# LN1's first two features of the second half in a fixed VectorE order, and FFN2's last input difference behind LN2's last split

## The chip, the core and the metric

The kernel runs on one core of a Trainium2 chip. The core has a matrix engine (TensorE, PE in the profile; its weight loads are listed as PEld), a vector engine (VectorE, DVE), an activation engine (ScalarE, ACT), GpSimd (POOL), and a queue that issues transfers (SyncE, SP). Each engine works through its own list of instructions in order, and waits on semaphores for the others. The metric is the device time of one execution in microseconds (us); of several executions the median is taken.

## What is computed

One layer of a hybrid decoder trunk on 544 tokens: 512 of one prompt (the first 256 tokens are called the first half here, the other 256 with 32 sample tokens the second half, 288 columns) with a model width of 1024. All tokens share the weights.

```python
x = layer_norm(ALPHA * x + 0.5 * swiglu(x, p["ffn1_wg"], p["ffn1_wu"], p["ffn1_wd"]), p["ln1_g"], p["ln1_b"])
proj = x @ p["w_in"]
...
mix = jnp.concatenate([y_rwkv, y_conv], axis=-1) @ p["w_out"]
x = layer_norm(ALPHA * x + mix, p["ln2_g"], p["ln2_b"])
x = layer_norm(ALPHA * x + 0.5 * swiglu(x, p["ffn2_wg"], p["ffn2_wu"], p["ffn2_wd"]), p["ln3_g"], p["ln3_b"])
```

Between `proj` and `mix` stand a per-token recurrence over a matrix state in eight heads (RWKV-7), and a short gated convolution. `layer_norm` subtracts the mean over the width, divides by the standard deviation, multiplies by g and adds b.

## The kernel before

Activations lie with the width on the 128 partitions: eight tiles of 128 features, called features 0 to 7 here, each with 544 token columns. `z` is the residual in f32. Every f32 product is made of three passes on PE: an operand is split into a high part (`hi`, a copy that ACT rounds) and a low part (`lo`, the difference, on DVE), and PE multiplies weight-high by high, weight-high by low and weight-low by high. `split` (L139 to L141) makes both parts of an activation; `wsplit` (L134 to L137) does it for a weight. `xhl` holds both parts of the input of the next matrix product. `mm3` (L148 to L156) is the inner loop of such a product: for each feature k three matmuls (L152, L153, L154), 256 columns wide in the first half and 288 in the second.

The work around LN1: FFN1 ends, LN1 of the first half runs while PE is busy with FFN1, and LN1 of the second half runs while PE makes the first half of five projections. PE then goes on with the second half of the projections 0, 1, 2 and so on, which need `xhl` of the second half. In the compiled order PE interleaves the first three of them (three accumulators, `mm`), taking for each feature the three passes of each projection.

`layer_norm` (L215) works on one half. Its last part, for the second half of LN1 (`fine` and `both` are set), treats features 0 and 1 singly: a multiplication by the reciprocal deviation (L269), scale and shift on DVE (L270), then the `sink`, which splits the feature into `xhl` and writes z to DRAM (`to_x`, L302). Features 2 to 7 go in pairs: one multiplication for the pair (L275), scale and shift of the odd feature on DVE (L279) and of the even one on ACT (L281), then the sink.

LN2 of the second half has no single features. It runs while PE makes FFN2's first products, and FFN2's input differences (`Ffn.inputs`, L454) follow it on DVE: FFN2 uses a scheme of fewer block products, for which differences of blocks of `z` are formed (`nt1`, L463; `ta`, L464, L466 and L469) and split into `tv`. `nt1` for features 0 and 1 and for features 2 and 3 stand in `cpb`; both are split into `xhl` at the end.

After the projections the first head pair is prepared: `project` mixes each projection with that of the token before (L914, L918), `gates`, `square`, `norms` (L996 clamps the key norms `kq`), `decays` and `prep` follow, and `scores` multiplies the score products by masks (L1060).

What sets the order: the kernel is written as generators that yield what they cost; `weave` runs one of them and fills in pieces of others by factors in the table `FILL`. A scheduler then lays out each engine's list from the recorded instructions by their dependencies and costs. `after(a, b)` adds a dependency without a semaphore: a stands behind b in the order; `tc.issue_after` does the same for all that is recorded in its block.

## Time and profile before

| | |
|---|---|
| median of 3 runs | 1072.5 us (1072.36 to 1072.72) |
| profiled execution, whole | 1072.43 us |
| profiled execution, span from first to last instruction | 1070.7 us |
| mean granted TensorE clock | 0.998 |
| instructions | 22612 |
| LN1 of the second half, last part | about 387 to 395 us |
| first pair's preparation | about 405 to 431 us |
| LN2 of the second half and FFN2's inputs | about 712 to 745 us |

The profile is of one execution. A row of the timeline gives the start in us from the span's start, the duration in us, engine, line, operation, output and inputs by the program's names, the shape and how many such instructions; where an engine stood idle ahead of it, the brackets give for how long and which instruction on which engine ended it. Instructions that follow each other on an engine can overlap by a few hundredths. The ends of matmuls are modelled.

### The profile page before, as it was taken

The numbers are of one execution on the slowest core, as the hardware profiler recorded it, in microseconds if no ns is written. First come the engines' busy times: TensorE is split into PE (matmuls) and PEld (weight loads), VectorE is DVE, ScalarE is ACT, GpSimd is POOL, SyncE is SP. The second block draws the span as 40 slices with busy tenths as digits, with TensorE's granted clock in tenths as the row PEclk, the third lists the DMA queues.
The fourth block names the chain that finished last, engine by engine and source line by source line (L and its number), as shares of the span: only waits on it lengthen the run. The fifth ranks groups of instructions, "written<-read, shape, count | busy, mean of one in ns | idle before, by whom it ended". The sixth has DMA issues, their size and how long they took to land.

```text
span 1070.7 us, 22612 instructions
## 1 busy us (share of the span) xinstructions
PE 1050.7 (98%) x9178; PEld 1010.5 (94%) x9178; DVE 844.7 (79%) x1557; ACT 583.2 (54%) x1070; POOL 154.9 (14%) x273
## 2 busy tenths in 40 slices
PE   9999999999999999999999999999999999999997
PEld 8999999999999999899889988999999999999996
DVE  6797888979875777793578657988979888797757
ACT  5746555555553668654444435767555555555524
POOL 0111121211200022133101200001211212121000
PEclk9999999999999999999999999999999999999999
DMA  8558585676854233324145724434766848668512
GB/s 292 132 112 186 120 199 135 145 172 132 186 118 158 79 88 109 85 82 99 41 143 161 173 81 139 141 119 79 152 165 137 200 101 194 143 137 189 147 43 84
DMA packets 91528, 144.48 MB, mean 135 GB/s; under 512 B 34848, under 2 KB 52384, under 8 KB 91296
## 3 DMA queue, kind: packets, MB, share of 16 engines
q1 hardware_dynamic: 68144, 110.76, 34.2%
q0 software_dynamic: 22848, 31.72, 19.2%
q8 instruction: 72, 1.18, 0.4%
q10 hardware_dynamic: 432, 0.56, 0.2%
q14 instruction: 32, 0.26, 0.1%
HBM read 128.81 MB, written 9.75 MB: 129 GB/s over the span
## 4 chain that ended last, share of the span: by engine, by line
PE 76%; DVE 13%; ACT 7%; issue 2%; DMA 2%; POOL 0%; ACTq 0%; DVEq 0%; SPq 0%
PE mm L553 9%; PE mm L554 9%; PE mm L555 9%; PE sm L553 6%; PE sm L554 6%; PE sm L555 6%; PE mm L152 6%; PE mm L153 5%; PE mm L154 5%; DVE hhl L141 2%; ACT hl L135 2%; DVE hl L136 2%; PE sm L441 1%; PE sm L1166 1%; PE mm L784 1%
## 5 line engine op out<-in xcount | busy, mean ns | idle before, releaser
L136 DVE TENSOR_TENSOR hl<-raw,hl 128x1024 fp32r<-128x1024 f32 (+3 forms) x230 | 270.2, 1179 | 63.7 <-ACT hl L135 62.6
L135 ACT ACTIVATE hl<-raw 128x1024 fp32r<-128x1024 f32 (+3 forms) x230 | 232.9, 1020 | 69.7 <-DVE raw L519 43.5
L152 PE MATMUL mm<-xhl,hl 128*128 128x256 f32 (+1 forms) x704 | 209.2, 299 | 0.5 <-ACT xhl L140 0.5
L153 PE MATMUL mm<-xhl,hl 128*128 128x256 f32 (+1 forms) x704 | 203.0, 289 | 0.4 <-DVE xhl L141 0.4
L154 PE MATMUL mm<-xhl,hl 128*128 128x256 f32 (+1 forms) x704 | 202.0, 287 | 0.0
L152 PEld LDWEIGHTS mm<-xhl,hl 128*128 128x128 f32 x704 | 132.0, 188 | 6.9 <-issue 2.0
L153 PEld LDWEIGHTS mm<-xhl,hl 128*128 128x128 f32 x704 | 132.3, 188 | 2.7 <-issue 1.0
L154 PEld LDWEIGHTS mm<-xhl,hl 128*128 128x128 f32 x704 | 132.3, 188 | 0.3 <-issue 0.2
L555 PE MATMUL sm<-xhl,hl 128*128 128x272 f32 x432 | 125.2, 290 | 0.0
L554 PE MATMUL sm<-xhl,hl 128*128 128x272 f32 x432 | 124.4, 288 | 0.0
L553 PE MATMUL sm<-xhl,hl 128*128 128x272 f32 x432 | 124.1, 287 | 0.0
L553 PE MATMUL mm<-tv,hl 128*128 128x272 f32 x288 | 83.3, 289 | 0.3
L555 PE MATMUL mm<-tv,hl 128*128 128x272 f32 x288 | 83.4, 290 | 0.0
L554 PE MATMUL mm<-tv,hl 128*128 128x272 f32 x288 | 83.1, 288 | 0.0
L553 PEld LDWEIGHTS sm<-xhl,hl 128*128 128x128 f32 x432 | 81.4, 188 | 0.0
L554 PEld LDWEIGHTS sm<-xhl,hl 128*128 128x128 f32 x432 | 81.3, 188 | 0.0
L555 PEld LDWEIGHTS sm<-xhl,hl 128*128 128x128 f32 x432 | 81.2, 188 | 0.0
L532 POOL DMA_DIRECT2D raw<-in_wd x32 | 39.2, 1462 | 288.0 <-DVE hlb L141 225.2
L526 POOL DMA_DIRECT2D raw<-in_gu x36 | 43.3, 1203 | 203.5 <-DVE hlb L141 143.8
L553 PE MATMUL mm<-hhl,hl 128*128 128x272 f32 x192 | 56.4, 300 | 0.3
L554 PE MATMUL mm<-hhl,hl 128*128 128x272 f32 x192 | 55.9, 291 | 0.8 <-DVE hhl L141 0.2
L553 PEld LDWEIGHTS mm<-tv,hl 128*128 128x128 f32 x288 | 54.2, 188 | 1.9 <-ACT cpb L620 1.9
(416 smaller groups left out, 2716.0 us busy)
## 6 DMA issues: line engine op xcount, KB each, us to landing
raw<-in_gu SPq DMA_DIRECT2D x84, 512.0 KB, 4.5
raw<-in_gu POOLq DMA_DIRECT2D x36, 512.0 KB, 6.6
raw<-in_wd SPq DMA_DIRECT2D x32, 512.0 KB, 4.5
raw<-in_win SPq DMA_DIRECT2D x26, 512.0 KB, 3.6
raw<-in_wd POOLq DMA_DIRECT2D x32, 256.0 KB, 6.0
z<-sv POOLq DMA_DIRECT2D x16, 272.0 KB, 8.4
raw<-in_wo_c SPq DMA_DIRECT2D x8, 512.0 KB, 3.6
raw<-in_wd SPq DMA_DIRECT2D x8, 384.0 KB, 3.2
```

Source lines behind the costliest of these rows:

```text
L135: seen["hi"] = ACT.activation(hl[:, 0, a:b], raw[:, a:b], AF.Copy)
L136: seen["lo"] = DVE.tensor_tensor(hl[:, 1, a:b], raw[:, a:b], hl[:, 0, a:b].bitcast(F32), op=OP.subtract)
L141: return DVE.tensor_tensor(lo, x, hi.bitcast(F32), op=OP.subtract)
L152: PE.matmul(out, wh, src[:, 0, k, c0:c1], start=(start and i == 0), stop=False)
L153: PE.matmul(out, wh, src[:, 1, k, c0:c1], start=False, stop=False)
L154: seen["fill"] = PE.matmul(out, wl, src[:, 0, k, c0:c1], start=False, stop=(stop and i == n - 1))
L441: PE.matmul(o[i][h][:, :c1 - c0], block(hl, v, k), xhl[:, y, k, c0:c1], start=(k == 0 and j == 0), stop=(k == KD - 1 and j == 2), skip_gro ...
L526: POOL.dma_start(x.rearrange("p (s c) -> p s c", s=2), bass.AP(tensor=a11.tensor, offset=a11.offset, ap=[[2 * D, P], [P * 2 * D, 2], [1, 5 ...
L532: POOL.dma_start(four(x)[:, i], bass.AP(tensor=a11.tensor, offset=a11.offset, ap=[[DFF, P], [P * DFF, 2], [1, 256]]), accum_op=OP.add)
L553: PE.matmul(out, wh, src(0, i), start=(first and i == 0), stop=False, skip_group_check=True)
L554: PE.matmul(out, wh, src(1, i), start=False, stop=False, skip_group_check=True)
L555: PE.matmul(out, wl, src(0, i), start=False, stop=(i == n - 1), skip_group_check=True)
```

## The change

In the last part of `layer_norm`, features 0 and 1 are put into a fixed order on DVE: feature 1's multiplication behind feature 0's scale and shift, feature 0's low part behind feature 1's multiplication, and feature 1's scale and shift behind feature 0's low part. The multiplication of a pair (in LN1's second half, all three pairs) stands behind feature 1's low part. `split` in `to_x` now leaves its last low part in `seen["xlo"]`. In `Ffn.inputs` the difference of features 2 and 3 stands behind that low part; FFN1's inputs run before any is set, so only FFN2's are touched. No instruction is added or removed.

```diff
-    seen = dict(rs=None, hhl=None, pe=None, fill=None, uv=None, new=[], old=[])
+    seen = dict(xlo=None, rs=None, hhl=None, pe=None, fill=None, uv=None, new=[], old=[])
...
         yield 1200 if pair else 600
+        los = []
         for d in range(2 if fine else 0):
             x = z[:, d, c0:c1]
-            DVE.tensor_tensor(x, x, rs[:, :n], op=OP.mult)
-            DVE.tensor_scalar(x, x, col(gcol, d), col(bcol, d), op0=OP.mult, op1=OP.add)
+            m = DVE.tensor_tensor(x, x, rs[:, :n], op=OP.mult)
+            if d:
+                after(m, ts)
+                after(los[0], m)
+            ts = DVE.tensor_scalar(x, x, col(gcol, d), col(bcol, d), op0=OP.mult, op1=OP.add)
+            if d:
+                after(ts, los[0])
             sink(d, z[:, d:d + 1, c0:c1], c0, c1)
+            los.append(seen["xlo"])
             yield 850
         for d in range(2 if fine else 0, KD, 2):
             zz = z[:, d:d + 2, c0:c1]
-            DVE.tensor_tensor(zz, zz, rs[:, None, :n].to_broadcast([P, 2, n]), op=OP.mult)
+            m = DVE.tensor_tensor(zz, zz, rs[:, None, :n].to_broadcast([P, 2, n]), op=OP.mult)
+            if los:
+                after(m, los[1])
...
-            split(xhl[:, 0, d:d + w, c0:c1], xhl[:, 1, d:d + w, c0:c1], x)
+            seen["xlo"] = split(xhl[:, 0, d:d + w, c0:c1], xhl[:, 1, d:d + w, c0:c1], x)
...
-                DVE.tensor_tensor(n1, z11[:, ks], z12[:, ks], op=OP.subtract)
+                e = DVE.tensor_tensor(n1, z11[:, ks], z12[:, ks], op=OP.subtract)
+                if k and seen["xlo"] is not None:
+                    after(e, seen["xlo"])
```

The change adds lines, so a line behind L266 stands up to 11 lines later in the changed kernel (L269 and L270 become L270 and L274, L275 becomes L282, L279 becomes L288, L463 becomes L472, L914 becomes L925).

DVE's list in the last part of LN1's second half, from feature 0's multiplication on (`z<-z,cpb` a multiplication, `z<-z,vc` scale and shift, `xhl<-z,xhl` a low part; 288 is one feature, 2x288 a pair). Before:

```order
L269 TENSOR_TENSOR z<-z,cpb 128x288 x2
L270 TENSOR_SCALAR z<-z,vc 128x288 x2
L275 TENSOR_TENSOR z<-z,cpb 128x2x288
L141 TENSOR_TENSOR xhl<-z,xhl 128x288 x2
L279 TENSOR_SCALAR z<-z,vc 128x288
L914 SCALAR_TENSOR_TENSOR v<-pb,vc,dt 128x256
L275 TENSOR_TENSOR z<-z,cpb 128x2x288
L141 TENSOR_TENSOR xhl<-z,xhl 128x2x288
L279 TENSOR_SCALAR z<-z,vc 128x288
L275 TENSOR_TENSOR z<-z,cpb 128x2x288
L279 TENSOR_SCALAR z<-z,vc 128x288
L141 TENSOR_TENSOR xhl<-z,xhl 128x2x288 x2
```

And now:

```order
L270 TENSOR_TENSOR z<-z,cpb 128x288
L274 TENSOR_SCALAR z<-z,vc 128x288
L270 TENSOR_TENSOR z<-z,cpb 128x288
L141 TENSOR_TENSOR xhl<-z,xhl 128x288
L274 TENSOR_SCALAR z<-z,vc 128x288
L925 SCALAR_TENSOR_TENSOR v<-pb,vc,dt 128x256
L141 TENSOR_TENSOR xhl<-z,xhl 128x288
L282 TENSOR_TENSOR z<-z,cpb 128x2x288 x2
L288 TENSOR_SCALAR z<-z,vc 128x288 x2
L282 TENSOR_TENSOR z<-z,cpb 128x2x288
L141 TENSOR_TENSOR xhl<-z,xhl 128x2x288 x2
L288 TENSOR_SCALAR z<-z,vc 128x288
```

Feature 0's low part moves ahead of the first pair's multiplication, feature 1's scale and shift behind it, and all three pairs' multiplications behind feature 1's low part; two of them now follow each other, ahead of the first pair's scale and shift. On PE, in the three interleaved projections (`mm_4547`, `mm_4554`, `mm_4619`), the matmuls that stand ahead of the first one on features 2 and 3 before (the second row that waits for ACT; the row that waits for DVE is the first on feature 2's low part):

```order
L153 MATMUL mm_4554<-xhl_68,hl_4354 128x288
L154 MATMUL mm_4554<-xhl_68,hl_4354 128x288
L152 MATMUL mm_4619<-xhl_68,hl_4397 128x288 [waits Activation_49]
L152 MATMUL mm_4547<-xhl_68,hl_4313 128x288 [waits Activation_49]
L152 MATMUL mm_4554<-xhl_68,hl_4354 128x288
L153 MATMUL mm_4619<-xhl_68,hl_4397 128x288
L154 MATMUL mm_4619<-xhl_68,hl_4397 128x288
L152 MATMUL mm_4619<-xhl_68,hl_4397 128x288
L153 MATMUL mm_4619<-xhl_68,hl_4397 128x288
L154 MATMUL mm_4619<-xhl_68,hl_4397 128x288
L152 MATMUL mm_4619<-xhl_68,hl_4397 128x288
L153 MATMUL mm_4547<-xhl_68,hl_4313 128x288 [waits DVE_49]
```

And now (the first row waits for feature 1's high part, the last but one for that of features 2 and 3):

```order
L152 MATMUL mm_4547<-xhl_68,hl_4313 128x288 [waits Activation_49]
L152 MATMUL mm_4554<-xhl_68,hl_4354 128x288
L154 MATMUL mm_4619<-xhl_68,hl_4397 128x288
L152 MATMUL mm_4619<-xhl_68,hl_4397 128x288
L153 MATMUL mm_4547<-xhl_68,hl_4313 128x288 [waits DVE_49]
L154 MATMUL mm_4547<-xhl_68,hl_4313 128x288
L153 MATMUL mm_4554<-xhl_68,hl_4354 128x288
L154 MATMUL mm_4554<-xhl_68,hl_4354 128x288
L153 MATMUL mm_4619<-xhl_68,hl_4397 128x288
L154 MATMUL mm_4619<-xhl_68,hl_4397 128x288
L152 MATMUL mm_4547<-xhl_68,hl_4313 128x288 [waits Activation_49]
L152 MATMUL mm_4554<-xhl_68,hl_4354 128x288
```

Now all 18 matmuls on features 0 and 1 stand ahead of the first on feature 2; before, the third projection's were taken partly behind it.

DVE's list in the preparation of the first head pair, before:

```order
L1005 SCALAR_TENSOR_TENSOR Pn<-keepm,sw 128x576
L996 TENSOR_SCALAR kq<-sm 128x256
L996 TENSOR_SCALAR kq<-sm 128x320
L914 SCALAR_TENSOR_TENSOR v<-pb,vc,dt 128x256
L918 SCALAR_TENSOR_TENSOR v<-pb,vc,dt 128x32
L1033 TENSOR_TENSOR AR_4714<-r,Pi 128x8x64
L1034 TENSOR_TENSOR AR_4714<-r,Pi 128x64
```

And now:

```order
L1016 SCALAR_TENSOR_TENSOR Pn<-keepm,sw 128x576
L1007 TENSOR_SCALAR kq<-sm 128x256
L925 SCALAR_TENSOR_TENSOR v<-pb,vc,dt 128x256
L929 SCALAR_TENSOR_TENSOR v<-pb,vc,dt 128x32
L1007 TENSOR_SCALAR kq<-sm 128x320
L1044 TENSOR_TENSOR AR_4714<-r,Pi 128x8x64
L1045 TENSOR_TENSOR AR_4714<-r,Pi 128x64
```

The second clamp of `kq` moves from ahead of the mixing of `v` to behind it, next to `AR`. The square of the keys that feeds these norms also moves ahead by a few instructions on ACT.

DVE's list at the end of LN2's second half (`cpb<-z` is the difference `nt1`; before, the first of the two is that of features 2 and 3). Before:

```order
L141 TENSOR_TENSOR xhl<-z,xhl 128x2x288
L279 TENSOR_SCALAR z<-z,vc 128x288 x2
L275 TENSOR_TENSOR z<-z,cpb 128x2x288
L463 TENSOR_TENSOR cpb<-z 128x544
L279 TENSOR_SCALAR z<-z,vc 128x288
L463 TENSOR_TENSOR cpb<-z 128x544
L141 TENSOR_TENSOR xhl<-z,xhl 128x2x288 x2
L405 TENSOR_TENSOR sv<-sv,mm 128x256
L141 TENSOR_TENSOR xhl<-z,xhl 128x2x288
L464 SCALAR_TENSOR_TENSOR cpb<-cpb,z 128x544
L141 TENSOR_TENSOR hlb<-raw,hlb 128x512
L141 TENSOR_TENSOR tv<-cpb,tv 128x544
```

And now:

```order
L141 TENSOR_TENSOR xhl<-z,xhl 128x2x288
L288 TENSOR_SCALAR z<-z,vc 128x288 x2
L282 TENSOR_TENSOR z<-z,cpb 128x2x288
L288 TENSOR_SCALAR z<-z,vc 128x288
L472 TENSOR_TENSOR cpb<-z 128x544
L141 TENSOR_TENSOR xhl<-z,xhl 128x2x288 x2
L414 TENSOR_TENSOR sv<-sv,mm 128x256
L141 TENSOR_TENSOR xhl<-z,xhl 128x2x288
L475 SCALAR_TENSOR_TENSOR cpb<-cpb,z 128x544
L141 TENSOR_TENSOR hlb<-raw,hlb 128x512
L472 TENSOR_TENSOR cpb<-z 128x544
L141 TENSOR_TENSOR tv<-cpb,tv 128x544
```

The difference of features 2 and 3 moves from ahead of three low parts and a scale and shift to behind the last low part and two more instructions, next to the low part of `tv`.

## The prediction

> **What bounds the kernel now.** I read the page first, then who waited for whom on TensorE, then the timelines of the three places that the change reorders.

> ```profile
> span 1070.7 us, 22612 instructions
> ...
> PE 1050.7 (98%) x9178; PEld 1010.5 (94%) x9178; DVE 844.7 (79%) x1557; ACT 583.2 (54%) x1070; POOL 154.9 (14%) x273
> ```

> TensorE (PE) is busy for 98% of the span, VectorE (DVE) for 79%, ScalarE (ACT) for 54%. A change on DVE can gain only where PE stands idle today, and costs only where it makes PE idle. So the question at each place is whether PE waits there, for whom, and by how much. Around the first layer norm (LN1) the list of PE's waits between 376 and 440 us has these rows (total, times, longest):

> ```profile
> PE mm L152 <- ACT xhl L140: 0.5, 1, 0.5
> PE mm L153 <- DVE xhl L141: 0.4, 1, 0.4
> PE sm L1091 <- DVE SC L1060: 0.3, 1, 0.3
> ```

> The first two lie where the change reorders DVE. In PE's own timeline (start in us, duration, engine, line, operands, count; in brackets the idle time ahead and who ended it):

> ```profile
> 387.71 0.28 PE L153 MATMUL mm<-xhl,hl 128*128 128x256 f32 x1
> 387.83 0.28 PE L154 MATMUL mm<-xhl,hl 128*128 128x256 f32 x1
> 388.60 0.53 PE L152 MATMUL mm<-xhl,hl 128*128 128x288 f32 x2 [0.50 <-ACT xhl L140]
> 389.50 0.40 PE L153 MATMUL mm<-xhl,hl 128*128 128x288 f32 x1 [0.37 <-DVE xhl L141]
> 389.74 0.29 PE L154 MATMUL mm<-xhl,hl 128*128 128x288 f32 x1
> ```

> The projections' first half ends at 387.83 + 0.28 = 388.11. The second half starts when feature 0's high part is there (388.60) and goes on when its low part is (389.50). A wait costs more than the idle time shown: that counts from the modelled end of the matmul ahead (387.71 + 0.28, while the next started at 387.83, 0.12 after it, 0.16 before that end), and after a wait the next matmul starts 0.24 later (389.50 to 389.74) and not 0.13. So 0.16 + 0.11 = 0.27 come on top of each. From 389.74 on there is no wait; matmul 58 of the 72 of the three interleaved projections starts here:

> ```profile
> 396.98 0.29 PE L154 MATMUL mm<-xhl,hl 128*128 128x288 f32 x1
> ```

> With (396.98 - 389.74 - 0.06 of one short stall) / 54 = 0.133 us a matmul, the last of the 72 starts at 396.98 + 14 x 0.133 = 398.84.

> **LN1, worked out step by step.** DVE and ACT before, in their timelines:

> ```profile
> 386.90 0.83 DVE L269 TENSOR_TENSOR z<-z,cpb 128x288 f32<-128x288 f32 x2 [0.31 <-ACT cpb L262]
> 387.65 0.76 DVE L270 TENSOR_SCALAR z<-z,vc 128x288 f32<-128x288 f32 x2
> 388.33 0.75 DVE L275 TENSOR_TENSOR z<-z,cpb 128x576 f32<-128x576 f32 x1
> 389.00 0.82 DVE L141 TENSOR_TENSOR xhl<-z,xhl 128x288 fp32r<-128x288 f32 x2
> ...
> 390.07 0.48 DVE L914 SCALAR_TENSOR_TENSOR v<-pb,vc,dt 128x256 f32<-128x256 f32 x1
> ...
> 392.14 0.76 DVE L275 TENSOR_TENSOR z<-z,cpb 128x576 f32<-128x576 f32 x1
> 392.94 0.43 DVE L279 TENSOR_SCALAR z<-z,vc 128x288 f32<-128x288 f32 x1
> ```

> ```profile
> 388.11 0.78 ACT L140 ACTIVATE xhl<-z 128x288 fp32r<-128x288 f32 x2 [1.24 <-DVE z L270]
> 388.80 0.37 ACT L910 ACTIVATE pb<-mm 128x256 f32<-128x256 f32 x1
> 389.06 0.47 ACT L913 ACTIVATE dt<-mm,omu 128x256 f32<-128x256 f32 x1
> 389.42 0.62 ACT L281 ACTIVATE z<-z,vc 128x288 f32<-128x288 f32 x1
> 390.25 0.69 ACT L140 ACTIVATE xhl<-z 128x576 fp32r<-128x576 f32 x1 [0.21 <-DVE z L279]
> ```

> How such rows are read: an independent DVE instruction starts 0.08 before the end of the one ahead (388.33 + 0.75 = 389.08, the next at 389.00); one that needs its result starts 0.04 after (392.14 + 0.76 = 392.90, the L279 that reads it at 392.94). From DVE to ACT or back takes 0.03. L269 takes (0.83 + 0.08) / 2 = 0.45, L270 0.43 as L279, a low part 0.45, a high part on ACT 0.44. I call L269 m, L270 s, the halves of a split hi and lo, and the normalization of features 2 and 3 (L275) M23. No operation is added or removed, the order alone moves:

> - m0 386.90 to 387.35, then s0 at 387.39 to 387.82 instead of 387.65 to 388.08. hi0 runs 387.85 to 388.29; PE can start at 388.34 instead of 388.60. lo0 is no longer behind M23: 388.32 to 388.78, before 389.00 to 389.45. PE goes on at 388.82 instead of 389.50, **0.68 us ahead**.
> - But s1 now stands behind lo0, and lo0 behind ACT's hi0: s1 388.69 to 389.12, hi1 389.15 to 389.59 (before, the second half of the ACT row at 388.11, done at 388.89), lo1 389.62 to 390.08. While DVE waits for hi1, v's mixing (L914) slips in: its input dt ends at 389.06 + 0.47 less the 0.6 by which pb and dt move up, 388.93.
> - M23 is held behind lo1: **389.99 to 390.75 instead of 388.33**. Behind it the scheduler puts M45, then both scalings (L279) of features 3 and 5. ACT scales feature 2 390.78 to 391.40, then feature 4 (it waits for M45, 391.42) 391.45 to 392.07, and only then makes hi23: 391.99 to 392.68, where the row says 390.25 to 390.94. That is 1.74 later. lo23 follows M67 and hi23: 392.71 to 393.47.

> PE has only features 0 and 1 to work on until then: 3 projections x 2 features x 3 matmuls = 18, so the 19th could start at 388.82 + 0.24 + 15 x 0.133 = 391.06. It starts **1.67 us** later, on hi23 (392.73), and 3 matmuls on lo23 costs 0.27 (393.51). The last 50 matmuls go on from 393.75; features 4 to 7 arrive in time (lo45 at 394.14, needed at 395.1; lo67 at 395.99, needed at 396.6). The last of the 72 starts at 393.75 + 49 x 0.133 = 400.27. Before it was 398.84: **+1.43 us on PE**. Put together: 0.68 gained, 1.67 + 0.27 lost with 2 x 0.11 for the restarts, less 0.05 of the short stall that goes.

> **What follows on the vector side.** The first of these projections ends 27 matmuls into the last stretch, at 397.2 instead of 396.2, so ACT's evacuation moves +1.0, and ACT (in the windows below the pair behind DVE's, 4.96 and 4.94 busy of 5.00 us) is full from there on. In the first pair's preparation the change also moves one clamp of the key norms (L996, 320 wide) from DVE's idle time to behind v's mixing:

> ```profile
> 400.00:405.00 5.00, 5.00 (x38) 4.35 (x37) 1.13 (x5) 4.96 (x12) 2.73 (x13) 1.00 0.65 203
> ...
> 410.00:415.00 5.00, 5.00 (x41) 5.00 (x41) 4.43 (x9) 4.94 (x9) 1.00 (x5) 1.00 0.17 24
> ```

> ```profile
> 410.50 0.48 DVE L914 SCALAR_TENSOR_TENSOR v<-pb,vc,dt 128x256 f32<-128x256 f32 x1 [2.17 <-ACT dt L913]
> ...
> 411.07 0.69 DVE L1033 TENSOR_TENSOR AR<-r,Pi 128x512 f32<-128x512 f32 x1
> ...
> 424.70 0.48 DVE L914 SCALAR_TENSOR_TENSOR r<-pb,vc,dt 128x256 f32<-128x256 f32 x1 [0.65 <-ACT dt L913]
> ...
> 425.27 0.48 DVE L996 TENSOR_SCALAR kq<-sm 128x320 f32<-128x320 f32 x1
> ...
> 427.53 2.68 DVE L1060 TENSOR_TENSOR SC<-sm,cs 128x512 f32<-128x512 f32 x5
> ```

> ```profile
> 430.07 0.24 PE L1091 MATMUL sm<-cs,v 64*64 64x64 f32 x1 [0.28 <-DVE SC L1060]
> ```

> Before, the clamp was in the 2.17 us that DVE idled ahead of 410.50; now it stands between v's mixing and L1033 and, 0.40 long (0.48 in the row of the second pair's, at 425.27, less the overlap), delays all behind it on a DVE that reaches the score masks (L1060) with little idle time. So the vector side comes +1.0 + 0.4 = +1.4 late to the wait at 430.07, PE +1.43: the 0.28 that PE waits there stays and absorbs nothing. If the clamp cost nothing the masks would come +1.0 and PE's wait there would shrink by what it is later, 0.4: +1.0 in all. That is the lower end, +1.4 the value I take, since of DVE's rows from 419 to the masks only the 0.65 ahead of 424.70 is idle, and that waits for ACT. After that PE's waits up to LN2 are short ones on answers to its own results, and shift with it.

> **LN2.** Second half, DVE, ACT and PE:

> ```profile
> 717.28 0.72 DVE L463 TENSOR_TENSOR cpb<-z 128x544 f32<-128x544 f32 x1
> ...
> 718.89 1.43 DVE L141 TENSOR_TENSOR xhl<-z,xhl 128x576 fp32r<-128x576 f32 x2
> ...
> 722.68 0.72 DVE L141 TENSOR_TENSOR tv<-cpb,tv 128x544 fp32r<-128x544 f32 x1
> ```

> ```profile
> 719.41 0.69 ACT L140 ACTIVATE xhl<-z 128x576 fp32r<-128x576 f32 x1
> ```

> ```profile
> 719.71 0.40 PE L153 MATMUL mm<-xhl,hlb 128*128 128x288 f32 x1 [0.41 <-DVE xhl L141]
> ```

> ```profile
> 749.33 0.39 PE L554 MATMUL mm<-hhl,hl 128*128 128x272 f32 x1 [0.17 <-DVE hhl L141]
> ```

> The input difference of features 2 and 3 (the L463 at 717.28, 0.64 net) no longer stands ahead of the splits. M67 ends at 717.36 (0.08 after the L463's start), s7 then runs 717.40 to 717.83, the other difference 717.75 to 718.47, and lo23 starts at 718.40 instead of 718.89 and ends at 719.15; nearly all of PE's wait (0.41 + 0.27, less 0.06 that stays) goes, 0.6. DVE, though, has the same work up to the FFN's first input: lo67 cannot start before hi67 ends (719.41 + 0.69 = 720.10), then L464 720.80, hlb 721.44, the moved difference 722.04 to 722.76, and tv's low part at 722.68, to the hundredth where it was. From there DVE's chain runs unchanged to the wait at 749.33, where PE already waits for DVE. What PE gains at 719.7 it waits for there: **0**, with -0.6 as the other end if that chain has slack that I don't see, and +0.1 if the difference ends later.

> **Sum.** LN1 +1.4 (+1.0 to +1.4), LN2 0 (-0.6 to +0.1). The profiled execution took 1072.43 us, 1.73 around its span of 1070.7; the median of the runs is 1072.5. Forecast: 1072.5 + 1.4 = **1073.9 us**, own range 1073.2 to 1074.3.

> **A rule weighed.** The stall of 1.67 (shown, counted from the modelled end, as 1.5) is longer than any wait of PE in the rows above. The tail of this execution shows what idling does to the granted clock (PE's last matmuls, then two windows; the clock stands ahead of the DMA share):

> ```profile
> 1061.72 2.05 PE L784 MATMUL sm<-hl,hhl 128*128 128x256 f32 x16
> ```

> ```profile
> 1065.40:1065.70 0.30, 0.00 (x0) 0.00 (x0) 0.30 (x2) 0.00 (x0) 0.00 (x0) 1.00 0.00 0
> ...
> 1065.90:1066.10 0.20, 0.00 (x0) 0.00 (x0) 0.20 (x1) 0.00 (x0) 0.00 (x0) 0.50 0.00 0
> ```

> PE ends at 1063.77, and at 1065.9 the clock is 0.50, hence half 2.0 to 2.1 us after it fell idle. The new stall, 1.5 counted in the same way, stays under that, with a short one close behind. [...]

> The rows show the drop after 2.0 us, so a rival with the clock in it stays.

> **Rivals.**
> 1. *Slower beyond the bound: the clock halves in the new stall.* For: two stalls, 1.67 + 0.27, within 2.5 us. Against: 0.5 us of matmuls lie between, and the row needed 2.0 without any. If PE then needs the same 2 us to get it back, it does half of 2.0: +1.0, 1074.9; twice that, 1075.9. It decides once a stall reaches 2 us.
> 2. *Smaller loss.* The clamp is free (+1.0) and LN2 keeps its 0.6: +0.4, 1072.9. Against: both rest on slack that the timelines don't show.
> 3. *Not slower: hi23 comes in time.* If ACT made hi23 before feature 4's scaling and M23 started by 388.4, the 18 matmuls would cover it: LN1 keeps its 0.68, and with LN2's 0.6 the time is 1072.5 - 1.3 = 1071.2. Against: both orders are fixed by the program. It decides once hi23 ends by 391.0, and 1.7 us are missing.
> 4. *The order is not what bounds*: 1072.5, if the moved instructions cost PE as much as they give.

> **How the numbers follow.** Forecast 0.60, rival 1 0.17, rival 2 0.14, rival 3 0.06, rival 4 0.03. Differences under 0.2% (2.1 us, 1070.4 to 1074.6) are about what a measurement of this kernel can tell from no change. The forecast and rivals 2 to 4 lie inside it; rival 1 outside, with a twelfth of the forecast for stalls that add up (0.05): slower 0.22. Faster needs more than all the waits named: 0.04. Within: 0.74. The range 1072.3 to 1075.2 takes in the forecast, rivals 2 and 4, and the lower part of rival 1.

> **What would show it.** Right: PE starts its second half near 388.3 and goes on near 388.8; a new wait for ACT's xhl, listed with about 1.5 us, near 391; a short one for DVE's lo23; the last of the 72 near 400.3; the wait at the masks still there; in LN2 no wait near 719.7 and about 0.8 instead of 0.17 at 749 (both plus 1.4). Wrong: hi23 before 391.5, a granted clock under 1 after 392, or a DVE chain in LN2 that starts tv's low part earlier than 1.4 after 722.68.

## The result, and the profile after

| | before | changed |
|---|---|---|
| runs beside each other, first comparison | 9 | 9 |
| median | 1072.72 us | 1075.58 us |
| lowest to highest | 1071.89 to 1073.69 | 1073.68 to 1077.37 |
| ratio of the times | | 1.0027 (95% interval 1.0018 to 1.0036) |
| the same, timed once more | 1072.88 (22 runs) | 1075.36 (11 runs), ratio 1.0018 (1.0009 to 1.0028) |
| profiled execution, whole / span | 1072.43 / 1070.7 | 1077.37 / 1075.6 |

The change makes the kernel slower by 2.5 to 2.9 us in the medians. The forecast was 1073.9, its range ended at 1075.2. What is left to explain is not only the median: the changed kernel's runs lie in steps, at 1073.7, about 1075.4 and about 1077.

PE's waits from 376 to 445 us of the changed kernel (total, times, longest), and then PE's timeline around the first:

```profile
PE mm L152 <- ACT xhl L140: 1.7, 2, 1.5
PE sm L1102 <- DVE SC L1071: 0.3, 1, 0.3
```

```profile
388.58 0.53 PE L152 MATMUL mm<-xhl,hl 128*128 128x288 f32 x2 [0.25 <-ACT xhl L140]
389.07 0.40 PE L153 MATMUL mm<-xhl,hl 128*128 128x288 f32 x1
...
391.17 0.29 PE L154 MATMUL mm<-xhl,hl 128*128 128x288 f32 x1
392.95 0.66 PE L152 MATMUL mm<-xhl,hl 128*128 128x288 f32 x3 [1.49 <-ACT xhl L140]
393.75 0.48 PE L153 MATMUL mm<-xhl,hl 128*128 128x288 f32 x1
394.03 0.44 PE L154 MATMUL mm<-xhl,hl 128*128 128x288 f32 x1
394.27 0.44 PE L152 MATMUL mm<-xhl,hl 128*128 128x288 f32 x1
```

The predicted stall is there. PE starts the second half at 388.58 and goes on at 389.07; after the 18th matmul (391.17) it waits 1.49 for ACT's high part of features 2 and 3 and starts again at 392.95. The wait of 0.37 for feature 0's low part is gone. All of this execution is 0.22 late before the change touches anything (feature 0's multiplication starts at 387.12 below, 386.90 before); less that, the times are 388.36, 388.85 and 392.73, where the prediction had 388.34, 388.82 and 392.73.

What the prediction did not have stands in the last two rows: from 394.03 on the matmuls are 0.24 apart and 0.44 long, not 0.133 and 0.29. The windows of the same trace (stretch, PE, PEld, DVE, ACT and POOL busy, then the granted clock, ahead of the share of the DMA queues) show why:

```profile
387.09:390.50 3.41, 3.16 (x23) 2.76 (x22) 3.09 (x8) 1.54 (x5) 0.90 (x4) 1.00 0.21 72
390.50:393.91 3.41, 1.79 (x12) 1.33 (x11) 3.41 (x7) 2.84 (x5) 0.56 (x1) 1.00 0.34 114
393.91:397.33 3.42, 3.42 (x15) 3.42 (x16) 1.55 (x3) 0.77 (x2) 0.00 (x0) 0.50 1.01 306
397.33:400.74 3.41, 3.41 (x28) 3.41 (x27) 0.42 (x2) 1.39 (x4) 0.31 (x2) 1.00 0.06 17
513.38:516.79 3.41, 3.41 (x42) 3.14 (x40) 2.37 (x5) 1.50 (x4) 0.00 (x0) 1.00 0.00 0
516.79:520.21 3.42, 3.42 (x96) 3.30 (x93) 0.91 (x4) 1.22 (x5) 0.57 (x2) 1.00 0.57 158
520.21:523.62 3.41, 3.41 (x22) 3.19 (x22) 0.73 (x3) 0.00 (x0) 0.00 (x0) 0.50 0.00 0
523.62:527.03 3.41, 3.41 (x67) 3.16 (x65) 1.62 (x6) 2.42 (x6) 0.57 (x2) 1.00 0.02 5
```

DVE and ACT at LN1, after:

```profile
387.12 0.46 DVE L270 TENSOR_TENSOR z<-z,cpb 128x288 f32<-128x288 f32 x1 [0.31 <-ACT cpb L262]
387.62 0.43 DVE L274 TENSOR_SCALAR z<-z,vc 128x288 f32<-128x288 f32 x1
387.96 0.45 DVE L270 TENSOR_TENSOR z<-z,cpb 128x288 f32<-128x288 f32 x1
388.56 0.46 DVE L141 TENSOR_TENSOR xhl<-z,xhl 128x288 fp32r<-128x288 f32 x1
388.93 0.42 DVE L274 TENSOR_SCALAR z<-z,vc 128x288 f32<-128x288 f32 x1
389.28 0.48 DVE L925 SCALAR_TENSOR_TENSOR v<-pb,vc,dt 128x256 f32<-128x256 f32 x1
389.87 0.46 DVE L141 TENSOR_TENSOR xhl<-z,xhl 128x288 fp32r<-128x288 f32 x1
390.25 1.42 DVE L282 TENSOR_TENSOR z<-z,cpb 128x576 f32<-128x576 f32 x2
391.58 0.77 DVE L288 TENSOR_SCALAR z<-z,vc 128x288 f32<-128x288 f32 x2
392.26 0.76 DVE L282 TENSOR_TENSOR z<-z,cpb 128x576 f32<-128x576 f32 x1
```

```profile
391.04 1.29 ACT L290 ACTIVATE z<-z,vc 128x288 f32<-128x288 f32 x2 [1.20 <-DVE z L282]
392.24 1.24 ACT L140 ACTIVATE xhl<-z 128x576 fp32r<-128x576 f32 x2
393.38 0.61 ACT L290 ACTIVATE z<-z,vc 128x288 f32<-128x288 f32 x1
```

The orders and the durations are those of the prediction's steps: M23 behind lo1 at 390.25, ACT scales features 2 and 4 (1.29) and makes hi23 only then, from 392.24. Less 0.22 that is 392.02, predicted 391.99. Further on, ACT's evacuation of the first of the three projections, before and after:

```profile
396.57 0.39 ACT L910 ACTIVATE pb<-mm 128x256 f32<-128x256 f32 x1 [2.29 <-PE mm L154]
```

```profile
399.35 0.39 ACT L921 ACTIVATE pb<-mm 128x256 f32<-128x256 f32 x1 [3.87 <-PE mm L154]
```

It is 2.78 later, 2.56 without the 0.22. The prediction had 1.0 here. The other 1.56 is the half-rate stretch: 3.42 / 0.24 = 14 matmuls, each 0.107 longer, is 1.5. On DVE the clamp of the key norms, now between v's mixing and the next product:

```profile
413.28 0.48 DVE L925 SCALAR_TENSOR_TENSOR v<-pb,vc,dt 128x256 f32<-128x256 f32 x1 [2.37 <-ACT dt L924]
413.68 0.24 DVE L929 SCALAR_TENSOR_TENSOR v<-pb,vc,dt 128x32 f32<-128x32 f32 x1
413.84 0.48 DVE L1007 TENSOR_SCALAR kq<-sm 128x320 f32<-128x320 f32 x1
414.24 0.68 DVE L1044 TENSOR_TENSOR AR<-r,Pi 128x512 f32<-128x512 f32 x1
```

v's mixing is 413.28 - 410.50 = 2.78 later, the product behind the clamp 414.24 - 411.07 = 3.17: the clamp costs 0.39. The wait at the score masks (L1102, 0.3 above) stays. Both as predicted. The recurrence's half-rate stretch adds another 1.5. This is ACT's evacuation of one of its steps, before and after:

```profile
541.38 0.28 ACT L1233 ACTIVATE W<-sm 128x128 f32<-128x128 f32 x1 [2.03 <-PE sm L1230]
```

```profile
546.08 0.28 ACT L1244 ACTIVATE W<-sm 128x128 f32<-128x128 f32 x1 [2.03 <-PE sm L1241]
```

It is 4.70 later; up to 503 us the shift is 3.18. At LN2 the DVE rows that the prediction speaks of:

```profile
723.31 1.42 DVE L141 TENSOR_TENSOR xhl<-z,xhl 128x576 fp32r<-128x576 f32 x2
...
727.60 0.72 DVE L141 TENSOR_TENSOR tv<-cpb,tv 128x544 fp32r<-128x544 f32 x1
```

```profile
754.24 0.39 PE L565 MATMUL mm<-hhl,hl 128*128 128x272 f32 x1 [0.29 <-DVE hhl L141]
```

Against a shift of 4.92 at LN2's start the last split starts 723.31 - 718.89 = 4.42 later, so 0.50 early, and tv's low part 727.60 - 722.68 = 4.92: the gain is gone there, to the hundredth. The span ends 4.9 later: 0.2 scatter, 1.0 LN1, 1.55 its half-rate window, 0.4 the clamp, 1.5 the second half-rate window, 0 at LN2, and 0.2 in small steps from 545 to 614 us.

### The profile page after: what moved, and what is told of

Its sections match the earlier page's. It is cut to its first block, busy times and chain, and to the rows that moved or that the text cites. A ratio compares the mean times of both kernels' runs of the same rounds, so it can differ in the third digit from the quotient of the medians.

```text
span 1075.6 us, 22611 instructions
## 1 busy us (share of the span) xinstructions
PE 1054.6 (98%) x9178; PEld 1013.8 (94%) x9178; DVE 845.0 (79%) x1557; ACT 583.6 (54%) x1070; POOL 153.6 (14%) x273
## 4 chain that ended last, share of the span: by engine, by line
PE 75%; DVE 14%; ACT 7%; issue 2%; DMA 2%; POOL 0%; ACTq 0%; SPq 0%; DVEq 0%
PE mm L564 9%; PE mm L565 9%; PE mm L566 9%; PE sm L564 6%; PE sm L565 6%; PE sm L566 6%; PE mm L152 6%; PE mm L153 5%; PE mm L154 5%; DVE hhl L141 2%; ACT hl L135 2%; DVE hl L136 2%; PE sm L450 1%; PE sm L1177 1%; PE mm L795 1%
## 5 line engine op out<-in xcount | busy, mean ns | idle before, releaser
L152 PE MATMUL mm<-xhl,hl 128*128 128x256 f32 (+1 forms) x704 | 210.4, 300 | 1.8 <-ACT xhl L140 1.7
L153 PE MATMUL mm<-xhl,hl 128*128 128x256 f32 (+1 forms) x704 | 204.5, 291 | 0.1
L154 PE MATMUL mm<-xhl,hl 128*128 128x256 f32 (+1 forms) x704 | 203.5, 289 | 0.0
L152 PEld LDWEIGHTS mm<-xhl,hl 128*128 128x128 f32 x704 | 133.0, 190 | 8.3 <-ACT xhl L140 2.2
L153 PEld LDWEIGHTS mm<-xhl,hl 128*128 128x128 f32 x704 | 133.6, 190 | 2.6 <-issue 1.0
L154 PEld LDWEIGHTS mm<-xhl,hl 128*128 128x128 f32 x704 | 133.8, 190 | 0.3 <-issue 0.2
```

Of the source, the lines that this page charges most:

```text
L152: PE.matmul(out, wh, src[:, 0, k, c0:c1], start=(start and i == 0), stop=False)
L153: PE.matmul(out, wh, src[:, 1, k, c0:c1], start=False, stop=False)
L154: seen["fill"] = PE.matmul(out, wl, src[:, 0, k, c0:c1], start=False, stop=(stop and i == n - 1))
```

## The experiments

Theory A, formed on these rows: the clock is decided in windows of 3.413 us which lie differently against the kernel in each run; when too few columns stream in a window, the next one runs at half rate and costs about 1.5. The measure of "too few" is the number of columns that its matmuls stream, as a share of 8192, which the expectations call the share of the time streamed. The 8192 is a unit that the author chose, not a pace that a run shows: 288 columns take 0.133 from start to start in the prediction's rows, which makes 7390 in 3.413 us. The window with the stall has about 10 matmuls of 288 columns, a share of 0.353. The window at 516.79 has 0.375. The lowest share in the kernel before that was not followed by a half-rate window is 0.376, at 512.86. So the limit was set at about 0.375. Moving such a window along the trace gives the positions at which it would be under that limit: in the kernel before about 0.28 of all positions near 513 us, 0.22 near 572 and 0.28 near 626; in the changed kernel the same, and 0.54 at LN1. So by theory A the kernel before has half-rate windows too, an estimated 0.28 + 0.22 + 0.28 = 0.8 a run, each behind one of these three places. The 0.54 is too high: the trace that it is read from has the half-rate stretch in it, and a window that reaches into the stretch looks thin because of it. In the trace of ln1_only below, with the same stall and the full rate behind it, the share at LN1 is 0.34. Theory B is that the stall's delay alone makes the loss.

All runs, in us. A half-rate window lowers a run's mean clock by 3.413 / 2 / 1073 = 0.0016, the end of the kernel by 0.001 to 0.002, so the last column counts the runs whose mean clock is under 0.998; it misses a few.

| kernel | runs | lowest | median | mean | clock under 0.998 |
|---|---|---|---|---|---|
| before, beside all experiments | 98 | 1071.99 | 1072.82 | 1073.14 | 24 |
| again (before, unchanged) | 11 | 1072.12 | 1073.46 | 1073.46 | 5 |
| changed, both times | 20 | 1073.68 | 1075.48 | 1075.65 | 13 |
| ln1_only | 11 | 1073.59 | 1075.53 | 1075.27 | 7 |
| ln2_only | 11 | 1072.02 | 1072.43 | 1072.85 | 2 |
| fill8, both times | 22 | 1073.44 | 1074.15 | 1074.40 | 5 |
| early_hi23 | 11 | 1072.71 | 1073.60 | 1073.81 | 2 |
| long | 5 | 1076.17 | 1076.28 | 1076.94 | 4 |
| long_fill | 6 | 1075.01 | 1076.11 | 1076.05 | 1 |
| best1 | 11 | 1072.18 | 1072.67 | 1072.83 | 0 |
| spread | 11 | 1073.02 | 1073.83 | 1073.78 | 1 |
| best2 | 11 | 1073.73 | 1074.20 | 1074.32 | 1 |
| fill_rec | 5 | 1076.74 | 1078.44 | 1078.18 | 5 |

### The parts, and the kernel before itself

**again** is the kernel before, unchanged.

> The kernel before, unchanged. [...] Theory B (only the new stall matters): no half-rate stretch before the end in any run of it, all runs within 1072.5 +- 0.5.

Its ratio is 1.0006 (0.9997 to 1.0015). Five of its 11 runs have a lower clock and stand at 1073.46 to 1075.23, as do 24 of the 98 other runs of the kernel before, with a mean of 1074.25 against 1072.77 of the rest. So the kernel before has half-rate windows too, 1.5 us each. The steps are blurred by a scatter of some 0.5, and its own two profiles fell on runs without one. The profile of ln2_only, whose LN1 and recurrence are in the order of before, shows one: the clock is 0.50 from 575.16 to 578.57, behind the place near 572.

**ln1_only** leaves out the dependency in FFN2's inputs, **ln2_only** all those in the layer norm:

```diff
-                if k and seen["xlo"] is not None:
-                    after(e, seen["xlo"])
```

> The LN1 part alone. If the whole loss is LN1's (stall +1.4, and half-rate windows behind it): as the changed kernel, 1073.9 without and 1075.6 with one half-rate window, median near 1075. If FFN2's moved difference has a share in the 2.9 us: below 1074.

> The LN2 part alone. My prediction's step: net 0, the times of the kernel before (1072.5, with the same scatter); PE's wait of 0.41 near 719.7 gone and DVE's chain behind it unchanged. Rival (the gain is kept): 1071.9. Rival (FFN2's part is what costs): above 1074.

The whole loss is LN1's: 1075.53 alone (ratio 1.0020, 1.0011 to 1.0029), and 1072.43 for LN2's part alone (0.9997, 0.9988 to 1.0006). The profile of ln1_only is worth as much as its times. PE's timeline, then the windows:

```profile
392.70 0.66 PE L152 MATMUL mm<-xhl,hl 128*128 128x288 f32 x3 [1.48 <-ACT xhl L140]
```

```profile
388.00:392.00 4.00, 2.97 (x19) 2.47 (x18) 3.75 (x9) 2.55 (x7) 1.35 (x3) 1.00 0.23 78
392.00:396.00 4.00, 3.17 (x22) 2.94 (x23) 3.19 (x6) 2.43 (x5) 0.00 (x0) 1.00 0.84 251
396.00:400.00 4.00, 4.00 (x33) 4.00 (x32) 1.26 (x4) 2.44 (x7) 1.01 (x4) 1.00 0.30 106
```

The stall is 1.48, the changed kernel's 1.49, and here the clock stays 1.00. The same stall lowers the clock in one execution and not in another: what differs is how it lies in the windows. Here they begin at 389.34 and 392.75 and are 0.47 and 0.77 full by the measure above; in the changed kernel the one that begins at 390.50 was 0.353 full. A rule by the stall's length can't tell these two apart.

### Filling the stall

**fill8** is the changed kernel with eight more matmuls ahead of the stall:

```diff
+            if fill and i == 1:
+                o = sm()
+                for _ in range(fill):
+                    PE.matmul(o[:, :c1 - c0], onr, src[:, 0, k, c0:c1], start=True, stop=True)
...
-        yield from mm3(q[:, :c1 - c0], w, xhl, range(KD), c0, c1)
+        yield from mm3(q[:, :c1 - c0], w, xhl, range(KD), c0, c1, fill=8 if h and not i else 0)
```

> The changed kernel with 8 more matmuls of 288 columns (1.06 us; their result is not used) among the 18 that PE has before the stall. DVE's and ACT's orders are those of the changed kernel. Theory A: the weakest window at LN1 rises from 0.246 of the time streamed to about 0.5, above 0.375, so the granted clock stays 1.00 from 380 to 410 in every run, the first three projections still end 1.4 later than before, and the times are 1073.9 plus what the three places of the recurrence add: mean 0.9 below the changed kernel's 1075.6. Theory B (the stall's delay of hi23 alone makes the loss, and the clock is not decided there): as the changed kernel, 1075.6.

PE's restart on hi23 and the windows of the changed kernel's stall, in fill8:

```profile
392.56 0.66 PE L152 MATMUL mm<-xhl,hl 128*128 128x288 f32 x3 [0.42 <-ACT xhl L140]
```

```profile
390.50:393.91 3.41, 2.86 (x20) 2.39 (x19) 3.41 (x8) 2.93 (x5) 0.17 (x1) 1.00 0.40 134
393.91:397.33 3.42, 3.42 (x28) 3.42 (x28) 1.16 (x3) 0.69 (x1) 0.00 (x0) 1.00 0.90 277
```

```profile
397.42 0.39 ACT L925 ACTIVATE pb<-mm 128x256 f32<-128x256 f32 x1 [2.33 <-PE mm L154]
```

0.42 of idle time is left, and hi23 comes when it came. The clock of 1.00 proves little in this one execution: its own windows begin at 389.81 and 393.22, and by ln1_only's trace the unfilled stall would have left the first of them 0.40 full there, just over the limit. What counts here are the times. ACT's evacuation stands at 397.42, 0.84 later than before; this execution is 0.17 ahead at LN1's start, so LN1 costs 1.01, the prediction's 1.0, and 1.22 behind the clamp is 0.39 more. The median fell to 1073.78 and the mean to 1074.11, 1.65 below that of the changed kernel's first nine runs (1075.77), more than expected. Nine and eleven draws scatter, so the two were timed once more on one chip.

> The changed kernel, unchanged, beside the next one on one chip. Theory A: lower cluster near 1073.8, and in some 8 of 10 runs 1.5 or 3.1 more; mean near 1075.5. Theory B (no share of the clock at LN1): the same mean as the kernel with filling matmuls.

> The changed kernel with 8 filling matmuls ahead of the stall, again. Theory A: lower cluster near 1073.8 as the changed kernel's, but only 3 to 5 of 10 runs above it, mean 1074.1 to 1074.4, 1.0 to 1.4 below the changed kernel of the same call. Theory B: the same mean as that.

The means are 1075.56 and 1074.69, beside 1073.40 of the kernel before in this call: the path costs 1.29, and the unfilled stall 0.87 more. An estimate of that from the traces: one grid of windows is walked through the trace of ln1_only (its half-rate stretch taken out) and through that of fill8, at all positions, and what follows a window under 0.375 is moved by 1.5. That gives 1.17 half-rate windows a run against 0.53, so 0.64 x 1.5 = 0.96. Of the 0.64, 0.34 are at LN1; the rest come in the recurrence, which the delay moves to other places in the windows. With the limit at 0.365 or 0.385 the estimate is 0.9 or 0.6. Over both times (20 and 22 runs) the difference of the means is 1.25 with a standard error of 0.31, and 13 of 20 runs against 5 of 22 have the lower clock. PE does more work and the kernel is faster: theory B can't give that.

### A shorter and a longer stall

**early_hi23** keeps the pairs behind feature 1's low part, but orders what follows:

```diff
             if los:
                 after(m, los[1])
+                if d > 2:
+                    after(m, s3)
...
+            if los and d > 2:
+                after(za, hi2)
```

Here s3 is the scaling of the odd feature of the pair ahead, za ACT's scaling of the even one and hi2 the high part ahead.

> The changed kernel, with features 3, 5 and 7 scaled on DVE straight behind their pair's multiplication, and ACT's high part of features 2 and 3 ahead of feature 4's scaling. The pairs still stand behind feature 1's low part. Theory A: hi23 comes 0.6 us earlier (392.24 in the changed kernel's row becomes about 391.6), the stall shrinks by as much, no window of 3.413 us at LN1 can stream less than 0.375, so no half-rate stretch there in any run; the key norms' clamp is back at its old place, which gives 0.4 back. Lower cluster of the times near 1073.0, mean about 0.5 above that. Theory B (holding the pairs behind feature 1's low part costs the 2.9 us as such): above 1075.

PE's waits in its timeline:

```profile
392.04 0.66 PE L152 MATMUL mm<-xhl,hl 128*128 128x288 f32 x3 [0.95 <-ACT xhl L140]
392.93 0.40 PE L153 MATMUL mm<-xhl,hl 128*128 128x288 f32 x1 [0.23 <-DVE xhl L141]
```

The stall is 0.95 and a wait of 0.23 for lo23 follows, which the expectation lacked. No position of a window is under the limit at LN1. In this execution a window begins at 390.32; by ln1_only's trace the stall of 1.48 would have left it 0.34 full, here it is 0.455 full and the clock stays 1.00. Two of 11 runs have the lower clock, and the mean is 1073.81, 0.6 over the kernel before of its call (1073.20): by ordering alone three quarters of the loss are gone.

**long** makes the stall longer, **long_fill** has 20 filling matmuls besides:

```diff
             if los:
                 after(m, los[1])
+                if d > 2:
+                    after(m, dly)
+                for _ in range(3 if d == 2 else 0):
+                    dly = DVE.tensor_scalar(zz, zz, 1.0, None, op0=OP.mult)
```

> The changed kernel with three multiplications by 1.0 (128x576) on DVE behind those of features 2 and 3, 0.76 each less overlap and with its dependency about 2.3 us together: hi23 and all behind it 2.3 later, the stall about 4.0 us. On the path 1073.75 (the lower cluster of the kernel with filling matmuls) + 2.3 = 1076.0. Theory A: 4 us without work leave at least one window of 3.413 us under 0.375 at nearly every position, sometimes two: a half-rate stretch behind LN1's stall in the profile, hardly any run near 1076.0, most at 1077.6, mean near 1078. Theory B (only the delay counts): 1076.0, and the scatter of the kernel before.

> The same with 20 matmuls of 288 columns whose result is not used (2.66 us) ahead of the stall. The orders on DVE and ACT are those of the kernel with the long stall. Theory A: the idle time left is about 1.3 us, no window under 0.375 at LN1, clock 1.00 from 380 to 410; lower cluster 1076.0, 3 of 10 runs above it, mean 1076.5, 1.5 below the kernel with the long stall though PE has more to do. Theory B: the same time as that kernel, or later.

Both sizes were wrong, since the delay was: three multiplications by a constant take 1.45 together, not 2.3.

```profile
391.04 1.45 DVE L288 TENSOR_SCALAR z<-z 128x576 f32<-128x576 f32 x3
```

```profile
394.45 0.67 PE L152 MATMUL mm<-xhl,hl 128*128 128x288 f32 x3 [2.95 <-ACT xhl L140]
```

The stall shown is 2.95. The mean is 1076.94 against 1076.05 with the filling, 0.9 apart, as expected in sign but not in size, and with 5 and 6 runs. Their profiles show the filling at work: in long the window from 391.63 is 0.105 full and the next one runs at half rate, in long_fill a window begins at 392.07 where by long's trace the unfilled stall would leave 0.26; it is 0.65 full, and the clock stays 1.00. Four of the 5 runs of long have the lower clock, one doesn't, at the same time as two that do (1076.28 beside 1076.17 and 1076.20). That one fits theory A badly; the scatter of single runs does not allow more.

### Other orders

**best1** takes LN1's features 0 and 1 in a better order, **spread** moves the samples' narrow matmuls apart, **best2** does both, **fill_rec** puts wide matmuls between the narrow ones.

```diff
-        when = {(2, 0): 1, (2, 1): 1, (2, 2): 1, (3, 0): 1, (3, 1): 1, (4, 2): 1, (5, 2): 2, (6, 2): 2}
+        when = {(2, 0): 1, (3, 0): 1, (3, 1): 1, (4, 0): 1, (4, 1): 1, (4, 2): 1, (5, 2): 2, (6, 2): 2}
```

That is spread; in best1 feature 1's multiplication stands behind s0, lo0 behind s1, M23 behind lo0, lo1 behind s3, and M45 behind lo1. In fill_rec:

```diff
+                if b in (2, 5):
+                    PE.matmul(q[:, 256:384], onr, onr, start=True, stop=True)
```

> LN1's order as m0, s0, m1, s1, lo0, M23, s3, lo1, M45 and hi23 ahead of feature 4's scaling on ACT, LN2's part kept. PE starts its second half 0.26 earlier than before, goes on 0.45 earlier, and hi23 is there at about 391.1, just in time. Expected: 0.2 to 0.4 faster than before on the path (lower cluster 1072.1 to 1072.3), the same scatter from the recurrence. Rival: pb and dt on ACT delay hi23, a stall of 0.3 eats the gain: 1072.5.

> The kernel before, with the second block of 32 narrow matmuls of the samples' step (8 columns each) and what follows it moved one step of the recurrence later, in both groups. Theory A: the weak places near 513 and 626 (0.28 of the positions each) go, since 2 us of narrow matmuls no longer stand together; what stays is 572. The lower cluster stays at 1072.5, and fewer runs stand 1.5 above it: about 2 of 10, against 15 of 44 so far of the kernel before. A theory in which the clock goes by idle time expects no change in that share: PE is shown busy there. If the moved steps lengthen the recurrence: lower cluster above 1072.8.

> best1 and spread together: lower cluster 1072.1 to 1072.3, about 2 of 10 runs 1.5 above it, mean 1072.5, that is 0.5 below the mean of the kernel before (1073.0).

> The kernel before, with two matmuls of 128 columns (result not used) in each of the four blocks of 32 narrow ones. Theory A: the weakest windows near 513 and 626 rise from 0.334 to about 0.396, over 0.375, so half-rate stretches stay only behind 572, in about 1 or 2 of 11 runs. Cost on the path: 4 x 0.06 us at each place, 0.5 in all, if nothing hides it, so lower cluster 1072.5 to 1073.0, and the mean between 1072.7 and 1073.3 against 1073.1 of the kernel before: a gain only if the recurrence waits there anyway.

best1 has hi23 in time, but its median of 1072.67 is the kernel before's (ratio 0.9997, 0.9988 to 1.0006): the gain of 0.2 to 0.4 did not come. In its profile small waits of 0.17 to 0.19 for the low parts stand at LN1, which takes 0.24 longer than before and not less, and another 0.4 comes between 520 and 570 us, which was not followed. None of its 11 runs has a lower clock, of which luck must be a part, since its recurrence is the old one. spread did to the scatter what theory A says: by its trace only 572 is left, 1 of 11 runs has a lower clock, and the standard deviation falls from 0.89 to 0.43. But it lengthens the recurrence by 0.5 to 0.7 in each group, and the lower cluster stands at 1073.0 to 1074.2, so nothing is gained (ratio 1.0005, 0.9997 to 1.0014, not told apart from 1). best2 adds the two and is slower (1.0012, 1.0003 to 1.0021). fill_rec was wrong altogether. PE's timeline in one block of the narrow matmuls:

```profile
513.72 0.52 PE L1293 MATMUL sm<-AR,DM 64*64 64x8 f32 x12
514.17 0.33 PE L1296 MATMUL sm<-ones 128*128 128x128 f32 x1
514.43 0.52 PE L1293 MATMUL sm<-AR,DM 64*64 64x8 f32 x12
```

A single wide matmul between narrow ones takes 0.26 of PE's time (514.17 to 514.43), not the estimated 0.06 (128 columns at the 0.133 of 288). The rows show another shape of the array for it (128*128 among 64*64), which may be the cause; that was not tried. The weak stretch became longer by 1.5 and no denser; its profile has both places followed by half rate, and the time rose to 1078.44. No version beat the kernel before.

### The limit itself

Over the 15 profiles there are 4683 windows. Fourteen windows in which PE still worked were followed by half rate; their shares run from 0.105 to 0.378. Of all others one was lower than 0.376, at 0.366 in the kernel before near its end (1061.9, in the run again). The limit had been set on two of these profiles, so the other 13 are a test of it. By this measure it is 0.37 to 0.38. Some matmul records are missing and their ends are modelled; counted back from the ends, the columns of the two groups overlap between 0.375 and 0.406, so a few hundredths of doubt remain. The counts over many runs agree less well: with 0.375, one grid of windows walked through its trace gives the kernel before a half-rate window in 0.53 of the positions (0.47 with 0.365), and 24 of 98 have a lower clock. The column above misses some (35 of the 98 took over 1073.4); whether the positions are not evenly spread is open.

## Why the prediction was wrong, step by step

- **LN1's order, +1.43 on PE: right.** hi23 at 392.02 (391.99 predicted), the stall shown 1.49 (about 1.5), the evacuation +1.01 in fill8 (+1.0).
- **The clamp, +0.4: right**, 0.39 in fill8 and in the changed kernel; in early_hi23 the clamp is back at its old place and the shift is 0.62 at 407 and 0.61 at 432, without a step.
- **The masks' wait stays: right** (0.28 and 0.27).
- **LN2, net 0: right**, shown by ln2_only and by tv's low part. That PE would wait 0.8 near 749 was wrong: it waits 0.29. The net is 0 all the same; into which short gaps the other half went was not followed.
- **The sum takes the clock as unchanged: this step failed.** The prediction let a stall lower the clock only from 2.0 us on, read from the end of the kernel, where PE falls idle for good. A tail can't show that limit: by theory A the clock drops there at the end of whatever window is the first one too empty, and 2.0 us was this execution's position: it drops 4.5 us after PE's last matmul in the changed kernel's trace, and over the 15 profiles the drop comes 1.9 to 5.3 us after PE's last matmul, a spread of one window. What the runs showed in its place is a window 0.353 full at LN1, half rate for the next 3.413 us, and 1.56 more on the path; over all runs the mean is 1.25 above that with the stall filled.
- **Rival 1 was the right mechanism, with price and condition mis-sized.** It stood at +1.0 for one drop from 2.0 us on; it is +1.5 at about a third of all positions (0.34) with a stall of 1.5, and more behind it, since the delay moves the recurrence to other places in the windows. The stalls that add up (0.05 in the prediction) are only in part the case: the 1.49 and the slow restarts at 392.95 and 393.75 fall into one window, but the wait of 0.25 ends at 388.58, 1.9 before that window begins.
- **The range assumed a scatter that the before runs had shown only by luck.** Three runs within 0.4 us hid that the kernel before loses 1.5 in a quarter of its runs. The path alone would have been within the forecast: fill8's mean is 1.26 over the kernel before's, 1.4 predicted. The ends of the terms as stated (+0.4 to +1.5) add up to 1072.9 to 1074.0; the own range of 1073.2 to 1074.3 does not follow from them.

Rivals 2 to 4 fell: the clamp isn't free, LN2 keeps nothing, hi23 is not in time.

## What to carry to other kernels

A wait of PE is priced twice: by what it delays, and by whether it makes a window of 3.413 us thin, the length in this kernel's traces. Count the columns that stream in the worst window around a new stall, waits and narrow matmuls together; under about 3100 of them (0.38 of 8192), which is the limit that these traces gave, add what a half-rate window costs (1.5 here) times the share of positions at which that can happen, counted on a trace that has no half-rate stretch there. And before believing a median of three, look whether the kernel has such places already: its runs then lie in steps, and the mean over many tells more than the median.

## What was not expected of the hardware

- PE "busy" for all of 3.42 us (96 matmuls, most 8 columns wide) lowered the clock, and the same stall did so in one execution (1.49, the changed kernel) and not in another (1.48, ln1_only).
- A wide matmul among narrow ones cost 0.26, where 128 columns would take 0.06 at the 0.133 of 288 columns.
- A multiplication by a constant on 128x576 took 0.48 (1.45 for three in a chain), one with operands per partition 0.43 on half as many elements.
